# All 22 units of the up projection as seven products; the first two begin with their plain blocks

## The chip, the cores and the metric

One core of a Trainium2 chip runs one program. The metric is the time of one execution on the device, in microseconds (us); lower is better. The engines are named as in the profile: PE (matrix products; PEld is its weight load), DVE (vector), ACT (scalar), POOL, and SP, which here only issues DMAs. Each engine works through its own instructions in the order of the program and waits on semaphores for the others.

## The reference, cut to what matters

The kernel computes one layer over 1024 tokens of width 1024. The change lies in the last third: the residual stream after attention and retention is normed and modulated, and goes through a gated MLP with a depthwise convolution of width 3 over the tokens.

```
hx2 = _modulate(_rmsnorm(x, norm2_g[l]), sh2, sc2)
...
u = h @ w_up                       # (1024 x 1024) @ (1024 x 5632)
...
u = sum(up[:, i:i + n] * conv_w[i] for i in range(CONV_W)) + conv_b
a, val = jnp.split(u, 2, axis=-1)
return (jax.nn.silu(a) * val) @ w_down
```

## The kernel before

All large products are made in three matmuls each: an operand is split into a high part (a cast on ACT) and a low part (a subtraction on DVE), and high x high, high x low and low x high are summed in PSUM. `split` (L85 to L87) is that pair of instructions; a block of 128x512 weights that is to be used has to be loaded, cast and subtracted.

The 5632 columns of `w_up` are worked in 22 units of 2 x 128 columns, 128 of the gate branch and 128 of the value branch with the same number. `seq` gives their order: unit 0 is column block 0, unit 1 is block 11, unit 2 is block 1, and so on. A unit is a 2 x 2 block product: two branches by two halves of the depth (a11, a12 for the gate; a21, a22 for the value) times the normed rows h, in two halves of the depth by two halves of the tokens (B11, B21 for tokens 0 to 511, B12, B22 for tokens 512 to 1023).

- A **plain** unit multiplies all of it: 2 branches x 2 token halves x 8 depth blocks x 3 = 96 matmuls of 128x512. Units 0 and 1 are plain (`PLAIN = 2`, `up`).
- A **seven-product** unit (class `Seven`, `Up`) needs 7 products of 4 x 3 = 12 matmuls, 84 in all. It uses the sums S1 to S4 of its four weight blocks, made on POOL (L1388 to L1391, in this order, S2 and S4 each from the one before), and the combinations T1 to T4 of the four blocks of h. The products gather in the banks X, Y and Z of PSUM, are copied or added to SBUF between (p1, u2, u3; L1413, L1416, L1422, L1403), and the finished unit goes through `conv`. Units 2 to 21 are of this kind, interleaved.

Ahead of it, `out_proj(tb)` makes the output projection of token block tb (8 blocks of 128 tokens), the residual rows x1 and their norm; `norm_out(tb)` turns the normed rows on PE (L1663, two groups of four transposes), modulates them and writes the high and low parts of h. They are called as `out_proj(tb)`, `norm_out(tb - 1)`. For blocks 0 to 3, h is also stored to DRAM (`d_h`). For blocks 4 to 7 it is read back into the tile vo, and four subtractions (L1678 to L1681) make this block's share of T1 to T4, which is stored to DRAM (`d_t`). Later `comb` loads these shares, four per T, and splits them into the tiles T.

The order: unit 0's products with tokens 0 to 511 follow `norm_out(6)`, then come block 7's transposes, unit 0's second half, unit 1, the loads and splits of T, and unit 2. The order of instructions on each engine is set by the framework's scheduler from the program as it is written. SP issues nearly all DMAs in one queue: a DMA that waits for its buffer or its data holds up those behind it. Raw weight blocks, raw T shares and the sums S of the seven-product units share a ring of 12 buffers (`ur_load`, `Up.raw`, tag "r").

Of the kernel before, what the change touches and what calls it, by code (L numbers as in the profile page):

```python
# [40 lines left out]
def tile_hybrid_layer(ctx, tc: tile.TileContext, io, dbg=None):  # L41
# [1581 lines left out]
    op = sb("outp", "right")  # L1623
# [6 lines left out]
    def out_proj(tb):  # L1630
        half, ts = tb // 4, slice((tb % 4) * P, (tb % 4 + 1) * P)
        x1 = op.tile([P, D], F32, tag="x1", bufs=3, name="x1")
        xr = op.tile([P, D], F32, tag="xn", bufs=2, name="xn")
        sync.dma_start(x1, io["x"][tb * P : (tb + 1) * P])
        for dh in range(2):
            cs = slice(dh * 512, dh * 512 + 512)
            m = po.tile([P, 512], F32, tag="o", bufs=2, name="om")
            for kb in range(KB):
                wc = wo[kb, dh]
                h_, l_ = mg[kb, half]  # L1640
                mm3(m, h_[:, ts], l_[:, ts], wc[:, 0], wc[:, 1], kb == 0, kb == KB - 1)
            vec.tensor_tensor(xr[:, cs], m, gate1[:, cs], ALU.mult)
            vec.tensor_tensor(x1[:, cs], xr[:, cs], x1[:, cs], ALU.add)
        sync.dma_start(d_x1[tb * P : (tb + 1) * P], x1)
# [3 lines left out]
        pool.tensor_tensor(ss[:, 1:2], ss[:, 0:1], mhalf[:, 0:1], ALU.pow)  # L1648
        vec.tensor_scalar(xr, x1, ss[:, 1:2], None, ALU.mult)
        return xr  # L1650

    def norm_out(tb, xr):
# [7 lines left out]
        for kg in range(2):  # L1660
            tp = po.tile([P, 4, P], F32, tag="t", bufs=2, name="tp2")
            for k in range(4):
                pe.transpose(tp[:, k], xr[:, (kg * 4 + k) * P : (kg * 4 + k + 1) * P], ident)  # L1663
            for k in range(4):
                kb = kg * 4 + k
                t = h2[half][kb]
                h_, l_ = (t[:, 0, ts], t[:, 1, ts]) if half == 0 else (t[0][:, ts], t[1][:, ts])
                a, sh = a2[:, kb : kb + 1], col[:, 24 + kb : 25 + kb]
                act.activation(h_, tp[:, k], AF.Identity, bias=sh, scale=a)
                v = vr[:, kb]  # L1670
# [6 lines left out]
        (b11, b21), (b12, b22) = [(t[:, : KB // 2], t[:, KB // 2 :]) for t in (vo, vr)]  # L1677
# [4 lines left out]
        for c, t in enumerate((b11, b22, b12, b21)):  # L1682
            sync.dma_start(d_t[c, tb - 4], t)
# [9 lines left out]
    def up(u, wu, half):  # L1693
        h = h2[half]
        hi, lo = ([t[:, i] for t in h] if half == 0 else [t[i] for t in h] for i in range(2))
        mm_a(u[:, half * 512 : half * 512 + 512], wu, lambda k: hi[k], lambda k: lo[k])

    def up_load(j, br):
        return [wload(io["w_up"][j, br, i]) for i in range(2)]

# [3 lines left out]
    early = []  # L1704
    for br in range(2):
        early.append((u_tile(br), up_load(0, br)))
        up(*early[br], 0)
    norm_out(NTB - 1, xr)
    po.release()
    pu.append(ps("u_ps1", "left"))  # L1710
    op.release()
    wop.release()
    gpool[1].release()

# [3 lines left out]
    tap = sb("conv", "right")  # L1718
    cw = tap.tile([P, 2 * NF, 3], F32, name="cw")
    sync.dma_start(cw, io["conv_w"])  # L1720
    cb = tap.tile([P, 2 * NF], F32, name="cb")
    sync.dma_start(cb, io["conv_b"])
# [50 lines left out]
    def u_out():  # L1773
        return tap.tile([P, T], F32, tag="uu", bufs=4, name="uu")

    def comb(c):
        t = [tpl.tile([P, 4, KH, P], F32R, name=f"T{c}{i}") for i in range(2)]
        for b in range(4):
            if b % 2 == 0:
                pair = u_out()  # L1780
            raw = pair[:, b % 2 * 512 : b % 2 * 512 + 512]
            sync.dma_start(raw, d_t[c, b])
            split(t[0][:, b], t[1][:, b], raw.rearrange("p (k t) -> p k t", k=KH))
        return t

    combs = {}

    class Up(Seven):
# [12 lines left out]
        def banks(self):  # L1801
            t = u_tile(2 * self.n)
            self.X, self.Y = t[:, 0:512], t[:, 512:1024]
            self.Z = u_tile(2 * self.n + 1)[:, 0:512]
            self.u = [u_out() for _ in range(2)]
# [11 lines left out]
        def c11(self):  # L1817
            act.copy(self.dst(0, 0), self.X)

        def done(self, b, half):  # L1820
            if (b, half) == (0, 1):
                conv(self.j, *self.u)
# [11 lines left out]
    seq = [j + NH * i for j in range(NH) for i in range(2)]  # L1834
    PLAIN = 2
    units = [Up(n, j) for n, j in enumerate(seq)]
    units[PLAIN].load(with_vec)

    for n, j in enumerate(seq[:PLAIN]):
        us2 = []  # L1840
        for br in range(2):
            u, wu = (u_tile(2 * n + br), up_load(j, br)) if n else early[br]
            for half in range(2) if n else (1,):
                up(u, wu, half)
            us2.append(u)
        for c in ((1, 0), (2, 3))[n]:
            combs[f"T{c + 1}"] = comb(c)
        conv(j, *us2)
    units[PLAIN + 1].load()
    for i, n in interleaved(PLAIN, NF):  # L1850
        units[i].step(n)
# [237 lines left out]
```

## Time and profile before

| what | us |
|---|---|
| median of 3 runs (lowest to highest) | 1763.57 (1760.81 to 1767.86) |
| the profiled execution | 1769.98 |
| its span | 1768.2 |
| last output product done, block 6 turned | 1108.41 |
| first matmul of a seven-product unit | 1154.18 |
| up projection's last matmul | 1547 |

All times in timeline rows are us from the start of the span. In a timeline row stand the start, the duration, the engine, the line, the operation, the tiles written and read, and the number of like instructions in a row; in brackets the idle time of the engine before it, and what ended it. The rows on which the prediction rests stand in it.

### The profile page before, as it was taken

What the parts mean: (1) busy time and instruction counts of PE and PEld (TensorE: products, weight loads), DVE (VectorE), ACT (ScalarE), POOL (GpSimd) and SP (SyncE); (2) the same over time, 40 slices, a digit from 0 to 9 for tenths busy, and PEclk for the clock granted to TensorE, in tenths of its full rate; (3) what the DMA queues carried; (4) which work ended last, traced back from release to release, by engine and by line L of the source; (5) the groups of instructions that cost most, each with busy time, mean ns of one, the idle gap of its engine ahead of it and who ended that gap; (6) DMA issues with size and microseconds to landing.
All of it is one profiled execution on the core that took longest, in us unless ns stands there. A gap on an engine that the chain in (4) does not pass through costs nothing.

```text
span 1768.2 us, 24667 instructions
## 1 busy us (share of the span) xinstructions
PE 1722.8 (97%) x8357; PEld 1429.4 (81%) x8357; DVE 1305.5 (74%) x2458; ACT 851.4 (48%) x1833; POOL 571.0 (32%) x477
## 2 busy tenths in 40 slices
PE   8699999999999999999999999999999999999997
PEld 3588888888888888788888888878888888788886
DVE  4878888765776766777675557878899899876655
ACT  5666666653443434453444324534444444554444
POOL 2510000002233343555422400145555655111444
PEclk9899999999999999999999999999999999999999
DMA  9133433433232212576658643723322332586753
GB/s 345 48 118 118 125 111 121 141 101 124 75 91 59 81 39 81 171 244 229 215 186 296 216 150 140 258 101 98 111 90 91 119 119 90 167 298 192 243 167 148
DMA packets 139551, 261.61 MB, mean 148 GB/s; under 512 B 15872, under 2 KB 28320, under 8 KB 139424
## 3 DMA queue, kind: packets, MB, share of 16 engines
q1 hardware_dynamic: 121504, 239.05, 41.2%
q10 hardware_dynamic: 17920, 20.98, 3.4%
q8 instruction: 66, 1.08, 0.3%
q14 instruction: 61, 0.50, 0.1%
HBM read 187.87 MB, written 69.48 MB: 146 GB/s over the span
## 4 chain that ended last, share of the span: by engine, by line
PE 44%; issue 5%; POOL 3%; DVE 3%; DMA 1%; ACT 1%; SPq 0%; POOLq 0%; ACTq 0%; DVEq 0%
PE u L1374 29%; PE y L1374 4%; PE pr L111 2%; PE pr L110 2%; PE pr L112 2%; PE om L121 1%; PE om L123 1%; PE om L122 1%; POOL x L1903 1%; PE pn L112 1%; PE pn L110 1%; PE pn L111 1%; DMA vo<-d_h 1%; DVE wc L87 0%; DMA uu<-d_t 0%
## 5 line engine op out<-in xcount | busy, mean ns | idle before, releaser
L1374 PE MATMUL u<-T,wc 128*128 128x512 f32 x960 | 228.6, 394 | 4.2 <-ACT pu L1413 2.6
L1374 PEld LDWEIGHTS u<-T,wc 128*128 128x128 f32 x960 | 181.2, 190 | 45.9 <-ACT pu L1413 5.9
L1374 PE MATMUL y<-wc,ahl 128*128 128x512 f32 x924 | 212.1, 391 | 2.9 <-DVE wc L87 1.8
L1374 PEld LDWEIGHTS y<-wc,ahl 128*128 128x128 f32 x924 | 174.4, 189 | 40.2 <-DVE wc L87 2.5
L87 DVE TENSOR_TENSOR wc<-ur,wc 128x512 fp32r<-128x512 f32 x137 | 124.6, 911 | 62.0 <-ACT wc L86 62.0
L86 ACT CAST wc<-ur 128x512 fp32r<-128x512 f32 x137 | 85.1, 622 | 126.9 <-PE y L1374 72.1
L111 PE MATMUL mm<-low,wc 128*128 128x512 f32 (+1 forms) x328 | 123.9, 378 | 0.0
L1374 PE MATMUL u<-h2a,wc 128*128 128x512 f32 x480 | 112.4, 389 | 0.7 <-DVE pu L1422 0.7
L110 PE MATMUL mm<-hx,wc 128*128 128x512 f32 x264 | 107.4, 407 | 0.3 <-DVE vc L221 0.3
L1374 PEld LDWEIGHTS u<-h2a,wc 128*128 128x128 f32 x480 | 90.0, 188 | 19.8 <-DVE pu L1422 1.2
L112 PE MATMUL mm<-hx,wc 128*128 128x512 f32 x264 | 105.0, 398 | 0.0
L86 ACT CAST wc<-s 128x512 fp32r<-128x512 f32 x80 | 49.7, 622 | 90.4 <-PE u L1374 87.4
L1513 POOL TENSOR_TENSOR col<-col,bcol 128x32 f32<-128x32 f32 x1 | 0.3, 253 | 282.2 <-DVE aw L538 282.2
L123 PE MATMUL mm<-wc,low 128*128 128x512 f32 (+1 forms) x240 | 91.3, 380 | 0.0
L1374 PE MATMUL u<-hxT,wc 128*128 128x512 f32 x384 | 89.6, 389 | 0.0
L87 DVE TENSOR_TENSOR wc<-s,wc 128x512 fp32r<-128x512 f32 x80 | 84.4, 1055 | 5.4 <-ACT wc L86 5.1
L1374 PEld LDWEIGHTS u<-hxT,wc 128*128 128x128 f32 x384 | 72.1, 188 | 15.0
L87 DVE TENSOR_TENSOR wc<-raw,wc 128x512 fp32r<-128x512 f32 x92 | 68.8, 757 | 17.1 <-ACT wc L86 17.0
L121 PE MATMUL mm<-wc,hx 128*128 128x512 f32 x192 | 75.2, 392 | 0.6 <-ACT r L1105 0.6
L122 PE MATMUL mm<-wc,hx 128*128 128x512 f32 x192 | 75.2, 392 | 0.0
L86 ACT CAST wc<-raw 128x512 fp32r<-128x512 f32 x92 | 56.7, 621 | 32.3 <-DMA raw<-in_w_pret 6.8
L87 DVE TENSOR_TENSOR wc<-wr,wc 128x512 fp32r<-128x512 f32 x56 | 54.2, 972 | 21.7 <-ACT wc L86 21.5
(393 smaller groups left out, 4693.2 us busy)
## 6 DMA issues: line engine op xcount, KB each, us to landing
ur<-in_w_up SPq DMA_DIRECT2D x80, 256.0 KB, 2.9
ur<-d_a SPq DMA_DIRECT2D x77, 256.0 KB, 3.4
aw<-in_w_ada SPq DMA_DIRECT2D x32, 512.0 KB, 3.2
pj<-in_w_down SPq DMA_DIRECT2D x44, 256.0 KB, 4.4
d_w<-pj SPq DMA_DIRECT2D x44, 256.0 KB, 2.0
d_a<-sa SPq DMA_DIRECT2D x44, 256.0 KB, 2.0
ur<-d_w SPq DMA_DIRECT2D x44, 256.0 KB, 3.6
d_a<-at SPq DMA_DIRECT2D x33, 256.0 KB, 2.8
```

The source lines that it names most:

```text
L86: act.copy(hi, src)
L87: (lo_eng or vec).tensor_tensor(lo, src, hi.bitcast(F32), ALU.subtract)
L110: pe.matmul(out, wh, xh, start=k == 0, stop=False)
L111: pe.matmul(out, wh, xl, start=False, stop=False)
L112: pe.matmul(out, wl, xh, start=False, stop=k == n - 1)
L121: pe.matmul(out, ah, bh, start=first, stop=False)
L122: pe.matmul(out, ah, bl, start=False, stop=False)
L123: pe.matmul(out, al, bh, start=False, stop=last)
L1374: pe.matmul(out, a, b, start=first and n == 0, stop=last and n == 2, skip_group_check=True)
L1513: pool.tensor_tensor(col[:, 16:48], col[:, 16:48], bcol[:, 16:48], ALU.add)
L1903: pool.tensor_tensor(z, z, fg[:, gs(dh)], ALU.mult)
```

## The change

Units 0 and 1 become seven-product units too. They begin with what needs only tokens 0 to 511: `early_plain` makes a11 x B11 in bank X, copies it (p1), and adds a12 x B21 in the same bank, for unit 0 and then for unit 1. The weight blocks for these two products are loaded and split ahead, through `wload`. Then `units[0].load()` loads the four blocks again for the sums, `norm_out(7)` turns block 7 into the free bank Z of unit 0, and its share of T1 to T4 is split where it is made, without going through DRAM. The other twelve shares are loaded through the ring of 12 buffers (before, through tiles of the convolution) and split, and `units[1].load()` follows. `open` copies the finished part in bank X to the unit's result (c11) and makes S4 x B22 in that bank; `close` makes the four products with T1 to T4 and the sums that differ by this order. The five remaining products of units 0 and 1 are written alternating, with unit 2's first product among them.

In `norm_out`, the group of depth blocks 4 to 7 comes first, and for tokens 512 to 1023 the depth blocks 0 to 3 are no longer split (no product uses them plain any more): ACT writes them to v in one instruction each. The tile x1 has two buffers in place of three.

```diff
-        x1 = op.tile([P, D], F32, tag="x1", bufs=3, name="x1")
+        x1 = op.tile([P, D], F32, tag="x1", bufs=2, name="x1")
...
-            h2[1] = [(gtile(0, F32R, "h2h"), gtile(0, F32R, "h2l")) for _ in range(KB)]
+            h2[1] = [None] * KH + [(gtile(0, F32R, "h2h"), gtile(0, F32R, "h2l")) for _ in range(KH)]
...
-        for kg in range(2):
-            tp = po.tile([P, 4, P], F32, tag="t", bufs=2, name="tp2")
+        for kg in (1, 0):
+            tp = banks[kg].rearrange("p (k t) -> p k t", k=4) if banks else po.tile([P, 4, P], F32, tag="t", bufs=2, name="tp2")
...
+                if t is None:
+                    act.activation(v, tp[:, k], AF.Identity, bias=sh, scale=a)
+                    continue
...
         for c, t in enumerate((b11, b22, b12, b21)):
-            sync.dma_start(d_t[c, tb - 4], t)
+            if banks:
+                split(combs[f"T{c + 1}"][0][:, tb - 4], combs[f"T{c + 1}"][1][:, tb - 4], t)
+            else:
+                sync.dma_start(d_t[c, tb - 4], t)
...
+    def early_plain(n):
+        X = early[n][0][:, 0:512]
+        early_prod(X, n, 0)
+        p1 = gtile(0, F32, "pu")
+        act.copy(p1, X)
+        early_prod(X, n, 1)
+        return p1
...
+        def open(self):
+            self.banks()
+            self.p1 = early_p1[self.n]
+            self.c11()
+            self.prod(self.X, self.s4, "B22", True, True)
+
+        def close(self, n):
+            if n == 0:
+                self.prod(self.Z, self.s1, "T1", True, True)
+            elif n == 1:
+                self.u2, self.u3 = (self.tmp() for _ in range(2))
+                self.prod(self.Y, self.s2, "T2", True, False)
+                vec.tensor_tensor(self.u2, self.Y, self.p1, ALU.add)
+                vec.tensor_tensor(self.u2, self.X, self.u2, ALU.add)
+                self.add(0, 1, self.Z, self.u2)
+            elif n == 2:
+                self.prod(self.Y, self.s3, "T3", False, False)
+                vec.tensor_tensor(self.u3, self.Y, self.p1, ALU.add)
+                self.add(1, 1, self.Z, self.u3)
+            else:
+                self.prod(self.Y, self.a22, "T4", False, True)
+                self.add(1, 0, self.Y, self.p1)
...
+    units[0].load()
+    for c in ("T1", "T2", "T3", "T4"):
+        combs[c] = [tpl.tile([P, 4, KH, P], F32R, name=f"{c}{i}") for i in range(2)]
+    norm_out(NTB - 1, xr, (early[0][1][:, 0:512], early[0][1][:, 512:1024]))
+    for c in (0, 1, 2, 3):
+        hi, lo = combs[f"T{c + 1}"]
+        for b in range(3):
+            raw = ur_load(d_t[c, b])
+            split(hi[:, b], lo[:, b], raw.rearrange("p (k t) -> p k t", k=KH))
...
+    units[1].load()
+    units[0].open()
+    units[1].open()
+    for i, n in ((0, 0), (1, 0), (0, 1), (1, 1), (0, 2), (0, 3), (1, 2), (2, -1), (1, 3)):
```

What this does to the order on three engines, at the start of the up projection. In the rows of the change, u_11859 and u_11860 are unit 0's banks (X and Y; Z), u_11903 and u_11904 unit 1's; xn_11760 are block 7's normed rows; wc is a split weight block, s a raw sum and ur a raw block.

PE in the change, from block 6's last transposes on:

```order
L1663 MATMUL tp2_11842<-ident_76,xn_11660 128x128 x4
L1374 MATMUL u_11859<-h2a_11035,wc_11863 128x512 x3
...
L1663 MATMUL u_11860<-ident_76,xn_11760 128x128 x4
L1374 MATMUL u_11859<-h2a_11039,wc_11882 128x512 x3
...
L1374 MATMUL u_11903<-h2a_11035,wc_11907 128x512 x3
...
L1374 MATMUL u_11903<-h2a_11039,wc_11926 128x512 x3
...
L1663 MATMUL u_11860<-ident_76,xn_11760 128x128 x4
L1374 MATMUL u_11859<-h2h_11614,wc_12085 128x512
...
L1374 MATMUL u_11903<-h2h_11614,wc_12103 128x512
L1374 MATMUL u_11903<-h2l_11615,wc_12103 128x512
L1374 MATMUL u_11860<-T10_11963,wc_12118 128x512
```

and before, where block 7 is turned behind 48 matmuls of unit 0:

```order
L112 MATMUL u_11926<-h2a_11042,wc_11934 128x512
L1663 MATMUL tp2_11964<-ident_76,xn_11784 128x128 x4
L1663 MATMUL tp2_11981<-ident_76,xn_11784 128x128 x4
L110 MATMUL u_11891<-h2h_11614,wc_11894 128x512
L110 MATMUL u_11926<-h2h_11614,wc_11929 128x512
```

Block 7's first group of transposes has moved from behind 48 matmuls to behind 12, its second group to behind 48; the products with h of tokens 512 to 1023 (h2h, h2l) now need S4 of units 0 and 1 (wc_12085, wc_12103).

ACT in the change, from the cast of unit 0's S4 to that of unit 1's (13 casts of T stand between block 7's four activations and the copy uu_12082):

```order
L86 CAST wc_12085<-s_11958 128x512
L1718 COPY pu_11922<-u_11903 128x512
...
L1670 ACTIVATE v_11971<-u_11860,col_83,a2_8902 128x128 x4
L86 CAST T10_11963<-ur_12018 128x512
L86 CAST T10_11963<-vo_11972 128x512
...
L86 CAST T40_11969<-ur_12046 128x512
L86 CAST T40_11969<-ur_12050 128x512
L1839 COPY uu_12082<-u_11859 128x512
L1839 COPY uu_12100<-u_11903 128x512
L86 CAST T40_11969<-ur_12054 128x512
L86 CAST wc_12103<-s_12077 128x512
L86 CAST wc_12118<-s_11955 128x512
```

and before, where the casts of T stand among the convolution of unit 0 and behind unit 2's first weight casts:

```order
L86 CAST wc_12330<-ur_12030 128x512
L86 CAST wc_12346<-s_12035 128x512
L1751 ACTIVATE ta_12123<-u_11891,cb_12024,cw_12022 128x1024
L86 CAST T10_12090<-uu_12092 128x512 x2
L1751 ACTIVATE at_12122<-u_11926,cb_12024,cw_12022 128x1024
```

Two copies out of PSUM (pu_11922, uu_12082) and the cast of unit 1's S4 now stand in one row with the casts of T.

SP in the change, from unit 0's first weight load on (d_x1 is the store of the residual rows, vo the read of `d_h`):

```order
L1738 DMA ur_11947<-in_w_up 128x512
L1659 DMA vo_11823<-d_h_65 128x1024
L1644 DMA d_x1_59<-x1_11759 128x1024
L1738 DMA ur_11949<-in_w_up 128x512
L1738 DMA ur_11951<-in_w_up 128x512
L1689 DMA d_t_66<-vo_11823 128x512
L1738 DMA ur_11953<-in_w_up 128x512
...
L1738 DMA ur_12050<-d_t_66 128x512
L1738 DMA ur_12054<-d_t_66 128x512
...
L1738 DMA ur_12066<-in_w_up 128x512
L1738 DMA ur_12068<-in_w_up 128x512
```

Unit 0's fourth block, A12 (ur_11953), stands behind a store of block 6's share of T1 (vo_11823); unit 1's blocks (ur_12066 and on) stand behind all twelve loads of T shares.

More of the change, by code (lines that the diff above doesn't have):

```diff
@@ L1818, in c11 @@
             act.copy(self.dst(0, 0), self.X)
+            self.done(0, 0)
         def done(self, b, half):
-            if (b, half) == (0, 1):
+            self.left -= 1
+            if self.left == 0:
                 conv(self.j, *self.u)
```

86 lines of the change are left out of this document (34 added, 52 removed).

## The prediction

> **What bounds the kernel now.** I read first the page's busy shares and its costliest groups, then the waits, then the stretch around the start of the up projection by windows and by timeline, TensorE's first.
>
> ```profile
> PE 1722.8 (97%) x8357; PEld 1429.4 (81%) x8357; DVE 1305.5 (74%) x2458; ACT 851.4 (48%) x1833; POOL 571.0 (32%) x477
> ...
> L1374 PE MATMUL u<-T,wc 128*128 128x512 f32 x960 | 228.6, 394 | 4.2 <-ACT pu L1413 2.6
> ```
>
> TensorE (PE) is busy 97% of the span: whoever saves time saves products, or closes one of the few places where PE stands. The changed stage has such a place.
>
> ```profile
> 1107.62 1.04 PE L1663 MATMUL tp<-ident,xn 128*128 128x128 f32 x8
> 1108.41 0.48 PE L110 MATMUL u<-h2a,wc 128*128 128x512 f32 x1
> ...
> 1156.90 0.61 PE L1374 MATMUL u<-T,wc 128*128 128x512 f32 x2
> 1159.06 0.73 PE L1374 MATMUL u<-T,wc 128*128 128x512 f32 x2 [1.55 <-DVE wc L87]
> 1162.40 10.23 PE L1374 MATMUL u<-T,wc 128*128 128x512 f32 x32 [2.60 <-ACT pu L1413]
> 1172.47 5.60 PE L1374 MATMUL u<-h2a,wc 128*128 128x512 f32 x24
> 1177.91 8.32 PE L1374 MATMUL u<-T,wc 128*128 128x512 f32 x36
> 1186.07 0.39 PE L1374 MATMUL u<-h2h,wc 128*128 128x512 f32 x1
> ```
>
> The timeline of PE. From 1177.91 to 1186.07, 36 matmuls take 8.16 us: **0.2267 us each** undisturbed, so a product of 12 matmuls is 2.72 us. From 1108.41 (first plain product) to 1172.47 PE did two plain units (192 matmuls), four products of the third (48) and 8 transposes (1108.41 - 1107.62 = 0.79): 240 x 0.2267 + 0.79 = 55.2 us of work in 64.06. **8.9 us are lost there**, in waits and in the clock:
>
> ```profile
> 1140.00:1162.40 22.40, 18.25 (x81) 14.46 (x79) 21.90 (x25) 16.17 (x26) 4.62 (x3) 0.98 0.52 169
> 1160.00:1165.00 5.00, 2.60 (x6) 2.12 (x7) 5.00 (x8) 2.57 (x4) 0.00 (x0) 0.63 0.61 193
> 1165.00:1170.00 5.00, 5.00 (x17) 3.90 (x17) 2.47 (x3) 0.67 (x2) 4.80 (x3) 0.68 0.47 174
> ```
>
> The windows (length, then busy time of PE, PEld, DVE, ACT, POOL, the granted clock, DMA): DVE is full (21.90 of 22.40) with the splits of the combinations T while PE waits, and after the wait the clock falls. The 32 matmuls from 1162.40 took 10.07 us where 7.25 were due: 2.8 us by the clock.
>
> **The change, part by part.** *Fewer products.* Two units go from 96 matmuls to 84: 24 x 0.2267 = **5.4 us less** on PE, the one certain gain. With the 8.9 us above it could be 14.3, if PE never stood. So I follow the new order of each engine through this stage, on before's clock, from 1108.41, where the first product on rows 0 to 511 can start in both kernels.
>
> *Wait 1, transposes.* Block 7's first four transposes stood behind 48 matmuls and now stand behind 12: PE reaches them at 1108.41 + 2.72 = 1111.1.
>
> ```profile
> 1083.87 0.25 PE om L123
> 1084.12 0.02 issue
> 1084.14 0.70 DVE xn L1642
> ...
> 1087.71 0.75 DVE xn L1649
> ```
>
> The chain from a block's last output product to its scaled rows takes 1088.46 - 1084.12 = 4.3 us when nothing is in its way. Block 7's last product ends at about 1107.8, so its rows are there at 1112.1 at the earliest; before's crowded DVE had them at 1113.28 + 0.75:
>
> ```profile
> 1113.28 0.75 DVE L1649 TENSOR_SCALAR xn<-x,ss 128x1024 f32<-128x1024 f32 x1 [0.44 <-POOL ss L1648]
> ```
>
> DVE is relieved of eight small instructions per block here, so I take 1112.3: PE waits 1.2 us (1.0 to 2.9). Four transposes (0.4) and the next 24 matmuls then end at 1118.1.
>
> *Wait 2, the bank of unit 1.* Its B21 product adds onto the bank that ACT must first copy (pu_11922), and in ACT's order that copy stands behind the cast of unit 0's S4. S4 is the last of four POOL sums and needs A12, whose load stands on SP behind a store of block 6's combinations, which wait for rows read back from DRAM.
>
> ```profile
> 1108.73 0.32 SPq L1683 DMA_DIRECT2D d_t<-vo  x1
> 1109.14 0.87 SPq L1727 DMA_DIRECT2D ur<-in_w_up  x2
> 1110.85 0.33 SPq L1644 DMA_DIRECT2D d_x<-x  x1
> ...
> 1111.27 6.10 DMA vo<-d_h
> ...
> 1123.30 3.25 DMA vo<-d_h
> ```
>
> ```profile
> ur<-in_w_up SPq DMA_DIRECT2D x80, 256.0 KB, 2.9
> ...
> d_w<-pj SPq DMA_DIRECT2D x44, 256.0 KB, 2.0
> ```
>
> The buffer vo comes free when block 5's store (1108.73) has landed, with the 2.0 us of the nearest store at 1110.7; the read takes 3.25 to 6.10: 1114.0 to 1116.8. The combination and the store's issue add about 1 us, A12's landing 2.9: 1118 to 1120.7. Beside that, the second weight block now stands behind the store of x at 1110.85: issued about 1111.7, landed at 1114.6 or later.
>
> ```profile
> 1130.16 1.61 POOL L1388 TENSOR_TENSOR s<-ur 128x512 f32<-128x512 f32 x1 [16.91 <-DVE vo L1681]
> ...
> 1134.67 1.73 POOL L1391 TENSOR_TENSOR s<-ur,s 128x512 f32<-128x512 f32 x1
> ...
> 1161.77 0.58 ACT L1413 COPY pu<-u 128x512 f32<-128x512 f32 x1
> ```
>
> The four sums take 1136.40 - 1130.16 = 6.2 us, so S4 is there between 1120.9 and 1122.5; I take 1122.0. ACT's cast (0.53, below) and copy (0.58) let B21 start at 1123.2: **PE waits 5.1 us** (3.9 to 5.6).
>
> *Wait 3, the bank of unit 0.* B21 and four transposes end at 1123.2 + 2.72 + 0.4 = 1126.3. The next product, B22 of unit 0, overwrites the bank that ACT copies into uu_12082. In ACT's order this copy stands behind four activations of block 7's other half and 13 casts of T.
>
> ```profile
> 1108.26 0.90 ACT L1669 ACTIVATE h2h<-tp,col,a 128x128 fp32r<-128x128 f32 x2 [2.36 <-PE tp L1663]
> 1144.84 3.73 ACT L86 CAST T<-uu 128x512 fp32r<-128x512 f32 x7
> 1141.29 2.49 DVE L87 TENSOR_TENSOR T<-uu,T 128x512 fp32r<-128x512 f32 x4
> 1149.61 7.60 DVE L87 TENSOR_TENSOR T<-uu,T 128x512 fp32r<-128x512 f32 x7
> ```
>
> 4 x 0.45 + 13 x 0.53 + 0.58 = 9.3 us: B22 starts at 1135.6, and **PE waits 9.3 us**. The last of these casts reads a buffer that DVE's split of an earlier T must free: DVE starts the combination at 1128.1, frees it at about 1129.5, the load lands 3 to 5 us later, inside the 13 casts. So the wait is 9 at the least, 11 with slow loads.
>
> *Wait 4, unit 1's weights.* All raw blocks share 12 buffers. Unit 0 still holds four, so unit 1's four weight loads come on SP behind the twelve T loads and wait for DVE's splits. From 1128.1 DVE has 18 instructions (4 combinations, 14 splits), at 2.49 / 4 = 0.62 us each with POOL idle. The buffer of the second weight load comes free behind the eleventh (so the order of the buffers has it) at 1128.1 + 11 x 0.62 = 1134.9; the load is issued at 1135.3 and lands 2.9 later, at 1138.2. POOL's sums take 5.2 (four at the 1.30 of a lone one) to 6.2, so S4 of unit 1 is there at 1144.0, cast at 1144.6. B22 of unit 0 was done at 1138.3: **PE waits 6.3 us** (4 to 8). Queued behind that cast on ACT are all the other weight casts, behind the T splits on DVE the weight splits, and on SP the loads of unit 2.
>
> ```profile
> 1133.42 1.30 POOL L1390 TENSOR_TENSOR s<-ur 128x512 f32<-128x512 f32 x1
> ```
>
> *After it.* At 1144.6 PE has done 60 of the first three units' 252 matmuls. Before had 36 of its 276 left at 1172.47. 156 x 0.2267 = 35.4 gives 1180.0. A restart after a stall cost before 2.8 us by the clock; I take the same: 1182.8, against 1172.47: **+10.3 us**. Weight splits (0.62 to 1.09 each, the last two rows above) keep ahead of products of 2.72: nothing more (0 to 2).
>
> *The clock after wait 2.* Before, the clock fell to half when PE had done four matmuls between 1157.5 and 1162.40. 5.1 us of standing should do the same, and B21's 12 matmuls at half clock push everything behind them by 2.7: **+13.0**. The Trainium skill, page "TensorE: Matmul & The Clock Gate", section "Part 1: The HAM clock gate (the "warmup" mystery)", asks for one whole idle window of about 3.4 us on a free-running grid; by that, 5.1 us holds such a window in about half of the phases, and the sum would be +10.3 or +13.0 by luck. The trace speaks for less than a whole window: two waits of 1.55 and 2.60 us with matmuls between them were enough. I keep +13.0.
>
> ```profile
> 1085.59 0.32 SPq L1644 DMA_DIRECT2D d_x<-x  x1
> ...
> 1107.41 0.68 DVE L1643 TENSOR_TENSOR x<-xn,x 128x512 f32<-128x512 f32 x1
> ```
>
> *At nothing:* one buffer of x fewer: block 7's load now waits for block 5's store, issued at 1085.59, and its rows are first used at 1107.41; the 22 us between, filled with block 6's and 7's output products, hide it (without that cover it would cost one load, some 4 us). Four DMAs fewer, and small norm instructions moved to ACT, which is 48% busy: nothing.
>
> Check: 1.2 + 5.1 + 9.3 + 6.3 = 21.9 new waits + 2.8 + 2.7 clock - 8.9 old losses - 5.4 = +13.1. The profiled execution (1769.98, span 1768.2) would be 1783; it was 6.4 above the median 1763.57, so I put the same difference on the median: **1777 us**, +0.75%.
>
> **The rivals.** *Not slower, the feed comes early* (other side): if unit 1's four loads went out before the T loads, S4 of both units were there by 1122, ACT's casts would be the only queue, and waits 3 and 4 shrink below the 8.9 us that before loses. At the best all waits go: -14.3, **1749**. It decides at new waits of 8.9 + 5.4 = 14.3. Against it: SP's order puts the loads behind, and ACT's 13 casts cannot end before 1135 unless block 7's transposes come earlier. *Early S4:* if A12 and the second weight block land by 1115, S4 is there at 1119.5; wait 2 is 2.6, the clock holds, and all behind comes 2.5 sooner: 10.3 - 2.5 = +7.8, **1771**, within 0.5%. For it: loads at 2.9 are a median. *Clock holds* after 5.1 us: +10.3, **1774**. *Slow splits:* at 7.60 / 7 = 1.09 us, if POOL runs beside them, 11 of them until the weights add 5: +18, **1782**.
>
> **How the numbers follow.** A difference of 0.5% (8.8 us, about what a measurement of this kernel can tell from none) starts at 1772.4. Forecast 0.38, clock holds 0.25, slow splits 0.10: slower together 0.73. Early S4, with other mixtures of shorter waits, 0.20 within 0.5%. The feed in time 0.07, faster. Range 1766 to 1785: above it only slow splits with more clock loss (0.05), below it the early feed and the lucky end of early S4 (0.12).
>
> **What would show it.** PE's count falls by 24. PE stands before the B21 of unit 1 (released by ACT's pu copy), before its first matmul on B22 of unit 0 (ACT's uu copy) and before B22 of unit 1 (ACT's cast of s), some 5, 9 and 6 us; the granted clock shows half speed behind the first or second of them; from unit 1's B22 on no wait is over 1 us. I am wrong if ACT's uu copy comes before 1131 on this clock, or if unit 1's S4 is there before 1138.

## The result and the profile after

The changed kernel takes **1783.56 us** (median of 4 runs, 1780.95 to 1786.32), the kernel before, run beside it, 1765.14 (4 runs, 1760.81 to 1767.86): ratio **1.0107**, 95% interval 1.0079 to 1.0135. A second series of runs gave 1784.33 against 1766.96, ratio 1.0092 (1.0070 to 1.0113). The change makes the kernel slower by about 1%, 12 to 24 us. The profiled execution took 1782.43 (span 1780.0), 12.4 more than that of before.

The page's first part, busy time of each engine:

```profile
PE 1722.8 (97%) x8333; PEld 1427.2 (80%) x8333; DVE 1309.6 (74%) x2444; ACT 853.6 (48%) x1843; POOL 581.7 (33%) x485
```

PE has 24 matmuls fewer, 5.4 us of work, and is busy just as long as before (1722.8), because other matmuls took longer. About 3 us of that is in the next rows: 5.8 us are lost there by slow matmuls, 2.8 in the prediction's rows of before. The rest lies outside these rows: ahead of them, with the same matmuls, PE was busy 1082.6 us here and 1079.4 before. The timeline of PE through the start of the up projection, after (start, busy time, instruction, in brackets the idle time ahead and what ended it):

```profile
1109.00 2.98 PE L1374 MATMUL u<-h2a,wc 128*128 128x512 f32 x12
1112.90 0.66 PE L1663 MATMUL u<-ident,xn 128*128 128x128 f32 x4 [0.92 <-DVE xn L1649]
...
1122.35 4.37 PE L1374 MATMUL u<-h2a,wc 128*128 128x512 f32 x12 [3.30 <-ACT pu L1718]
1126.56 0.60 PE L1663 MATMUL u<-ident,xn 128*128 128x128 f32 x4
1136.86 0.79 PE L1374 MATMUL u<-h2h,wc 128*128 128x512 f32 x1 [9.71 <-ACT uu L1839]
...
1146.14 0.79 PE L1374 MATMUL u<-h2h,wc 128*128 128x512 f32 x1 [3.79 <-ACT wc L86]
...
1150.64 15.57 PE L1374 MATMUL u<-T,wc 128*128 128x512 f32 x68
...
1559.99 20.34 PE L1374 MATMUL y<-wc,ahl 128*128 128x512 f32 x89
```

Four waits of 0.92, 3.30, 9.71 and 3.79 us, released by the four things that the prediction named, 17.7 us in all; behind them no wait in this stage is over 0.8 us. Behind three of the four the matmuls start at about half speed: the 12 of B21 take 4.21 us (1122.35 to 1126.56) where 2.72 are due, the 12 of unit 0's B22 5.49 (1136.86 to 1146.14 - 3.79), the 13 matmuls from 1146.14 to 1150.64 take 4.50 where 2.95 are due. That is 5.8 us more.

I call **the stage** the time from the first plain product to the long run of y products, the start of the down projection: 1559.99 - 1109.00 = 451.0 us here, 1546.90 - 1108.41 = 438.5 before (1546.90 is the row below). All of the profiled pair's difference of 12.4 us is in it (12.5).

```profile
1546.90 33.48 PE L1374 MATMUL y<-wc,ahl 128*128 128x512 f32 x147
```

Where VectorE stood meanwhile: windows of after, then of before (length, busy time of PE, PEld, DVE, ACT, POOL, granted clock, DMA):

```profile
1120.00:1140.00 20.00, 7.94 (x23) 6.18 (x24) 15.84 (x28) 12.70 (x25) 1.16 (x1) 0.72 0.74 251
1140.00:1160.00 20.00, 16.21 (x61) 12.68 (x60) 11.40 (x12) 5.71 (x10) 12.73 (x9) 0.86 0.38 121
```

```profile
1120.00:1140.00 20.00, 19.33 (x86) 15.53 (x85) 14.36 (x29) 8.89 (x16) 7.42 (x5) 1.00 0.67 229
1140.00:1160.00 20.00, 18.25 (x80) 14.46 (x78) 19.50 (x22) 14.07 (x22) 4.62 (x3) 1.00 0.52 171
```

In the changed kernel no engine is full in either 20 us: PE 7.94 of 20, DVE 15.84 and then 11.40. Everybody waits for somebody. Before, the plain products kept PE at work (19.33, 18.25) while DVE caught up on the splits of T. The chain of waits of after, followed from 1120 to unit 1's B22 (start, duration, what):

```profile
1121.31 0.60 DVE vo L1684
...
1121.94 2.00 DMA d_t<-vo
...
1123.95 5.24 DMA vo<-d_h
...
1129.27 0.70 DVE vo L1681
...
1137.40 2.95 DMA ur<-in_w_up
...
1144.22 1.23 POOL s L1391
```

Between the last DVE row and the weight load (ur) stand ACT's casts of T, and behind the sum s its cast (1145.47) and PE's matmul. This is one queue through VectorE, the DMAs, ScalarE and GpSimd, with PE as its last member. The prediction had one of its links in front of wait 2 but not here: there is a single buffer vo, so the stored rows with which block 7 is combined can be read back (5.24 us) only when block 6's last combination has been stored from it (2.00 us). But this link came last by only 0.5 us: the read landed at 1129.19, and ACT's four activations on block 7, behind PE's transposes, ended at 1128.69. ACT's timeline:

```profile
1127.19 1.50 ACT L1670 ACTIVATE v<-u,col,a 128x128 f32<-128x128 f32 x4 [0.85 <-PE u L1663]
1128.58 0.63 ACT L86 CAST T<-ur 128x512 fp32r<-128x512 f32 x1
1130.00 0.62 ACT L86 CAST T<-vo 128x512 fp32r<-128x512 f32 x1 [0.80 <-DVE vo L1681]
...
1136.24 1.05 ACT L1839 COPY uu<-u 128x512 f32<-128x512 f32 x2
```

From 1127.19 on stand four activations, 13 casts and the first uu copy, back to back but for the 0.80 us in which ACT waits for block 7's first combination. PE starts B22 behind that copy, at 1136.86.

### The profile page after: what moved, and what is told of

Read it like the earlier page. It is cut to its first block, busy times and chain, and to the rows that moved or that the text cites. A ratio compares the mean times of both kernels' runs of the same rounds, so it can differ in the third digit from the quotient of the medians.

```text
span 1780.0 us, 24636 instructions
## 1 busy us (share of the span) xinstructions
PE 1722.8 (97%) x8333; PEld 1427.2 (80%) x8333; DVE 1309.6 (74%) x2444; ACT 853.6 (48%) x1843; POOL 581.7 (33%) x485
## 3 DMA queue, kind: packets, MB, share of 16 engines
q8 instruction: 65, 1.06, 0.2%
## 4 chain that ended last, share of the span: by engine, by line
PE 44%; issue 5%; DVE 3%; POOL 3%; ACT 1%; DMA 1%; POOLq 0%; ACTq 0%; DVEq 0%; SPq 0%
PE u L1374 29%; PE y L1374 4%; PE om L121 2%; PE om L122 2%; PE om L123 2%; PE pr L111 2%; PE pr L110 2%; PE pr L112 2%; POOL x L1935 1%; PE pn L112 1%; PE pn L111 1%; PE pn L110 1%; DVE wc L87 1%; DVE ta L1763 0%; DVE at L1763 0%
## 5 line engine op out<-in xcount | busy, mean ns | idle before, releaser
L1374 PE MATMUL u<-T,wc 128*128 128x512 f32 x1056 | 248.5, 391 | 1.3 <-DVE pu L1416 0.8
L1374 PEld LDWEIGHTS u<-T,wc 128*128 128x128 f32 x1056 | 197.5, 188 | 46.1 <-ACT pu L1413 3.1
L1374 PE MATMUL u<-h2a,wc 128*128 128x512 f32 x528 | 126.0, 393 | 4.1 <-ACT pu L1718 3.3
L1374 PEld LDWEIGHTS u<-h2a,wc 128*128 128x128 f32 x528 | 99.7, 190 | 26.3 <-ACT pu L1718 3.7
L86 ACT CAST wc<-s 128x512 fp32r<-128x512 f32 x88 | 54.1, 621 | 103.7 <-PE u L1374 92.2
L87 DVE TENSOR_TENSOR wc<-s,wc 128x512 fp32r<-128x512 f32 x88 | 90.7, 1036 | 6.3 <-ACT wc L86 5.9
L1388 POOL TENSOR_TENSOR s<-ur 128x512 f32<-128x512 f32 x22 | 34.8, 1582 | 121.8 <-DVE wc L87 77.4
L1374 PE MATMUL u<-h2h,wc 128*128 128x512 f32 x176 | 60.9, 407 | 13.5 <-ACT uu L1839 9.7
```

Of the source, the lines that this page charges most:

```text
L86: act.copy(hi, src)
L87: (lo_eng or vec).tensor_tensor(lo, src, hi.bitcast(F32), ALU.subtract)
L1374: pe.matmul(out, a, b, start=first and n == 0, stop=last and n == 2, skip_group_check=True)
L1388: pin(pool.tensor_tensor(self.s1, self.a21, self.a22, ALU.add))
```

## The experiments

Theory Q (a queue): the time at which T and unit 1's S4 are fed decides, and PE's waits are only the places where that shows; taking one wait away lengthens the next. Its rivals: the waits add up (A), the clock makes the loss (C), T and VectorE's splits hold behind everything (D), GpSimd's sums and VectorE slow each other (V). Executions differ by some us ahead of the stage too, so the stage, taken from each kernel's profile, is the measure, beside the ratio of the timed runs to those of the kernel before:

| kernel | stage, us | ratio to before (95%) |
|---|---|---|
| before; once more (e12) | 438.5; 435.9 | |
| after; once more (e8) | 451.0; 453.0 | 1.0107 (1.0079 to 1.0135); 1.0092 (1.0070 to 1.0113) |
| e1 copy first | 453.2 | 1.0103 (1.0086 to 1.0120) |
| e2 blocks aside | 451.7 | 1.0087 (1.0070 to 1.0103) |
| e3 loads first | 449.3 | 1.0066 (1.0049 to 1.0082) |
| e4 clock kept | 451.4 | 1.0080 (1.0061 to 1.0098) |
| e5 = e2 + e3 | 448.9 | 1.0060 (1.0038 to 1.0083) |
| e6 = e5 + third unit | 446.0 | 1.0062 (1.0042 to 1.0083) |
| e7 = e6 + e1 + block 6 | 439.2 | 1.0034 (1.0018 to 1.0049) |
| e9 sums on VectorE | 446.3 | 1.0065 (1.0044 to 1.0085) |
| e10 = e7 + sums | 435.9 | 1.0023 (1.0010 to 1.0035) |
| e11 before + sums | 435.0 | 1.0004 (0.9989 to 1.0019) |

The stage comes from one profile of each run. Two executions of one kernel differ in it by 2.6 us (before) and 2.0 (after), so a difference of that size between two rows says little by itself.

### e1: unit 1's copy ahead of the cast (wait 2)

```
-        act.copy(p1, X)
+        early_copy.append(act.copy(p1, X))
...
-            self.prod(self.X, self.s4, "B22", True, True)
...
+            cast = act.copy(w[:, 0], self.s4)
+            tc.add_manual_dep(cast.ins, early_copy[1].ins.name, mybir.DependencyInfo(mybir.DependencyClass.NoSync, mybir.DependencyReason.DATA))
...
```

> Edit: on ScalarE, unit 1's bank copy (pu) goes ahead of the cast of unit 0's S4, so the second new wait has no cause any more. Theory Q (one queue: what counts is when the combinations T and the second S4 are fed; the time at which PE reaches its earlier products is not what holds): B21 of unit 1 starts by 1120 on the changed kernel's clock and at full clock, the wait of 3.3 us is gone, but the wait for the uu copy grows by what was won (9.7 to 12 to 14 us), since that copy stays behind the same T casts; the time changes by 0 to -2.5 us. Rival A (the waits add up one by one): -3.3 and the 1.6 us that B21 lost at half clock, -5 us.

Neither. The stage is 453.2, as long as in the changed kernel. ScalarE's timeline in e1:

```profile
1119.48 0.46 ACT L1673 ACTIVATE h2h<-u,col,a 128x128 fp32r<-128x128 f32 x1 [3.53 <-DVE v L1674]
1123.04 0.46 ACT L1673 ACTIVATE h2h<-u,col,a 128x128 fp32r<-128x128 f32 x1 [3.10 <-DVE v L1674]
1123.40 0.58 ACT L1718 COPY pu<-u 128x512 f32<-128x512 f32 x1
```

The cast no longer stands ahead of the copy, but two activations of block 7 do, which wait for VectorE, 3.53 and 3.10 us: the copy came at 1123.40, 13.6 us after the first product (1109.82), in the changed kernel 12.7 (1121.71 - 1109.00). So the edit did not do what it was made for, and it says nothing on A. What it shows is that the cast was not the only thing in ScalarE's row.

### e2: finished blocks copied aside (wait 3)

```
         early_prod(X, n, 1)
+        c0 = gtile(0, F32, "pu")
+        act.copy(c0, X)
+        early_c11.append(c0)
...
-            self.c11()
...
                 self.prod(self.Z, self.s1, "T1", True, True)
+                act.copy(self.dst(0, 0), early_c11[self.n])
+                self.done(0, 0)
```

> Edit: the finished upper left blocks of units 0 and 1 are copied aside right behind their second product into a spare buffer and moved to uu later, so B22 of unit 0 no longer waits for the uu copy behind the T casts (wait of 9.7 us). Theory Q: B22 of unit 0 runs by 1128 and then PE stands once, 14 to 17 us, for the cast of unit 1's S4, which stays near 1145.5; the time changes by -1 to +1 us. Rival A (the waits add up): -9.7 us and the 2.6 us that B22 of unit 0 lost at half clock, -12 us.

PE's timeline in e2:

```profile
1118.76 0.80 PE L1374 MATMUL u<-h2h,wc 128*128 128x512 f32 x1 [2.71 <-ACT wc L86]
...
1119.78 4.04 PE L1374 MATMUL u<-h2a,wc 128*128 128x512 f32 x12
...
1142.63 0.79 PE L1374 MATMUL u<-h2h,wc 128*128 128x512 f32 x1 [16.05 <-ACT wc L86]
```

The 9.71 us are gone, B22 of unit 0 is done by 1126.6, and PE stands 16.05 us for unit 1's S4. That wait ends 36.6 us after the first product (1106.01), in the changed kernel 37.1. Theory Q's numbers came out, and the stage is unchanged (451.7); A wanted 12 us.

### e3: unit 1's loads ahead of the T loads (wait 4)

```
     units[0].load()
+    units[1].load()
...
-            raw = ur_load(d_t[c, b])
+            raw = rawload(d_t[c, b]) if (3 * c + b) % 2 else ur_load(d_t[c, b])
...
-    units[1].load()
```

> Edit: unit 1's four weight loads and sums go out directly behind unit 0's, ahead of the T loads; every other T load lands in a buffer of the other stream of raw blocks, since the ring of 12 is full. Theory Q: S4 of unit 1 is cast by 1132 in place of 1145.5, the wait of 3.8 us behind B22 of unit 0 is gone, the wait for the uu copy (9.7) stays within 3 us of its size because ScalarE's T casts stay ahead of it, and up to 3 us of waits for T come anew; the time changes by -4 to -7 us. Rival D (the T splits on VectorE are the bound behind everything): the same wait comes back in front of the first T product, 0 to -2 us.

```profile
1122.12 4.81 PE L1374 MATMUL u<-h2a,wc 128*128 128x512 f32 x12 [5.57 <-ACT pu L1718]
...
1134.22 1.22 PE L1374 MATMUL u<-T,wc 128*128 128x512 f32 x2 [6.85 <-ACT T L86]
```

PE's timeline in e3. Unit 1's S4 is no longer waited for; wait 2 grew from 3.30 to 5.57, and T is waited for in place of the uu copy, 6.85 us and then 2.37 for its split on VectorE. The stage is 1.7 to 3.7 us shorter than in the two executions of the changed kernel, between D's 0 to 2 and Q's 4 to 7; by the medians, each against that of the kernel before beside it, the gain is 6 to 7 us, Q's. The two measures do not agree well enough to decide here.

### e4: the clock kept up through waits 3 and 4

```
         def open(self):
             self.banks()
...
+            for k in range((30, 22)[self.n]):
+                m = pe.matmul(early[1][1][:, 512:1024], w[:, 0, 0:P], w[:, 0], start=True, stop=True)
...
```

> Edit: 30 idle products into an unused half bank between block 7's last transposes and B22 of unit 0, and 22 ahead of B22 of unit 1 (matmuls that add no term of the result): PE is busy inside the third and fourth wait, and the clock should be full behind both. Theory Q: B22 of unit 0 ends 2 to 3 us sooner and the wait for unit 1's S4 takes that in; only B22 of unit 1 is won, which now takes 4.5 us for 12 products: -1.8 us. Rival C (the clock makes the loss): all that B22 of both units lose at half clock comes back, -4.4 us or more.

```profile
1136.36 0.50 PE L1374 MATMUL u<-h2h,wc 128*128 128x512 f32 x1 [2.65 <-ACT uu L1844]
...
1145.63 0.50 PE L1374 MATMUL u<-h2h,wc 128*128 128x512 f32 x1 [1.27 <-ACT wc L86]
...
1148.76 15.80 PE L1374 MATMUL u<-T,wc 128*128 128x512 f32 x69
```

Both B22 run at full clock, the 12 matmuls of the second in 3.13 us (1145.63 to 1148.76). But it starts 37.1 us after the first product (1108.56), to a tenth as in the changed kernel: what the first B22 won, the queue took. What is left, 1.1 us (1.55 lost behind wait 4 in the changed kernel, 0.4 here), did not show in the whole stage (451.4). By the medians, each against that of the kernel before beside it, e4 gains 3.4 to 4.5 us, with intervals that overlap, so how much of the time came back is not settled. Even C's full 4.4 us would be a quarter of the slowdown: C is out as the main cause. Of the 5.8 us that matmuls lost to the clock in the changed kernel, the 2.8 between waits 3 and 4 did not move unit 1's B22.

### e5, e6: two waits together, and more work for PE

e5 is e2's and e3's diffs together. e6 adds unit 2's two plain products in an unused half bank:

```
-        X = early[n][0][:, 0:512]
+        X = early[n][0][:, 0:512] if n < EARLY else early[1][1][:, 512:1024]
...
+    early_p1.append(early_plain(2))
...
```

> The edits of e2 (finished blocks copied aside) and e3 (unit 1's loads ahead of the T loads) together. Loss of PE is counted from the first plain product to the first product of the fourth unit (less 156 products of 0.2267 us and 0.8 us of transposes): 25.0 us in the changed kernel, 24.7 in e2, 22.5 in e3. Theory Q (one queue: ScalarE's T casts and the feed of unit 1's S4 each hide the other): together they win more than their sum of 2.8 us, 7 to 10 us, so a loss of 15 to 18 us and a time 7 to 11 us below the changed kernel's on this chip. Rival A (gains add): 2.8 us, loss 22.2. Rival D (what holds is that T is not ready, whatever else is ready): no more than e3's 2.5 us.

> e5, and the two plain products of unit 2 brought forward too (into an unused half bank), so PE has 24 more products that need no T. Theory Q: 24 products of 0.2267 us fill up to 5.4 us of what e5 still loses; since two of its waits lie ahead of them or come with their banks, 1 to 4 us less loss than e5. Rival D (T holds): the waits for T shrink by just what is brought forward, up to 5.4 us. Rival E (ScalarE's copies for the third unit delay its T casts): nothing, within 1 us of e5.

The expectation speaks of the fourth unit's first product; the 156 products that it counts end at that of the third (unit 2), and so it is counted here. In e5 that product starts at 1167.96, so the loss is 1167.96 - 1108.97 - 156 x 0.2267 - 0.8 = 22.8 us: 2.2 less than in the changed kernel, not 7 to 10. **Theory Q fails here**; A's sum of two small gains (2.8) and D's bound (2.5) both fit the number. PE's timeline and DVE's window in e5:

```profile
1133.61 0.51 PE L1374 MATMUL u<-h2h,wc 128*128 128x512 f32 x1 [1.31 <-ACT wc L86]
...
1140.96 12.11 PE L1374 MATMUL u<-T,wc 128*128 128x512 f32 x45 [1.53 <-DVE T L87]
1157.05 11.07 PE L1374 MATMUL u<-T,wc 128*128 128x512 f32 x36 [3.98 <-DVE pu L1822]
```

```profile
1140.00:1160.00 20.00, 15.05 (x52) 11.91 (x53) 19.95 (x25) 9.01 (x15) 9.98 (x7) 0.81 0.46 136
```

PE reaches unit 1's B22 12 us earlier than in the changed kernel (24.6 against 37.1 us after the first product), and then loses it: VectorE is full (19.95 of 20) with splits of T and of weights, so its sum out of the bank (L1822) comes late, PE stands 3.98 us for it, and the next 36 matmuls start at half clock (10.91 us to 1167.96 where 8.16 are due). Behind the queue stands VectorE's work: D in a wider form. In e6 the stage is 2.9 us shorter, within Q's 1 to 4; PE's 24 matmuls brought forward would fill time in which VectorE works. But by the medians the two are alike, and 2.9 is hardly more than two executions of one kernel differ: this gain is not shown.

### e7: everything, and block 6 split where it is made

e7 is e6 with e1's edit, and with block 6's `norm_out` moved behind unit 0's loads, where the tiles T exist already, and the plain products and unit 1's loads behind it:

```
-            if banks:
+            if tb >= NTB - 2:
                 split(combs[f"T{c + 1}"][0][:, tb - 4], combs[f"T{c + 1}"][1][:, tb - 4], t)
...
+    norm_out(NTB - 2, last)
...
-        for b in range(3):
...
+        for b in range(2):
...
```

> e6, and unit 1's bank copy ahead of the cast of unit 0's S4 (e1), and the combinations of block 6 split where they are made as well (no store and no read back of them; eight T loads instead of twelve). Theory Q: both the S4 casts and T come sooner; PE's loss from the first plain product to the first product of the fourth unit is 11 to 14 us, no wait over 2.5 us is left and the clock holds through the stage; the time is 10 to 15 us below the changed kernel's and within 0.3% of the kernel before. Rival F (VectorE is full there and slowed by GpSimd's sums, so more splits early push the rest back): no better than e6.

The stage is 439.2, 12 to 14 us shorter than in the changed kernel, the time 1772.08 against 1784.33. The loss up to unit 3's first product (1173.35, behind 228 products) is 10.8 us, where 11 to 14 was expected; but waits of 3.71 and 3.26 are left, and the clock drops once. DVE's windows say what holds now:

```profile
1120.00:1140.00 20.00, 15.40 (x62) 11.95 (x61) 19.96 (x30) 14.75 (x30) 6.83 (x5) 0.91 0.44 150
1140.00:1160.00 20.00, 18.60 (x80) 14.19 (x79) 17.86 (x23) 7.18 (x13) 14.74 (x8) 1.00 0.37 109
```

### e8 and e12: both kernels once more

> The changed kernel as it is, beside the others on one chip. If the gap of 12.4 us between the two profiled executions is the change's size, the ratio is 1.007 (+12 us); if the gap of the medians is, 1.0107 (+19 us).

> The kernel before once more, for a second profile of it. If the two waits of 1.55 and 2.60 us and the half clock behind them belong to the kernel, the stage is 438.5 us again, within 0.7; if they come and go from execution to execution, it is 3 us or more shorter here, which would explain why the medians lie 17 to 19 us apart and the first pair of profiled executions 12.4.

In e8 the four waits are there again (0.92, 3.19, 9.17 and 4.24 us), with other clock losses. PE at the second of them, and VectorE at block 7's first combination:

```profile
1121.35 5.49 PE L1374 MATMUL u<-h2a,wc 128*128 128x512 f32 x12 [3.19 <-ACT pu L1718]
1129.11 0.69 DVE L1681 TENSOR_TENSOR vo<-v,vo 128x512 f32<-128x512 f32 x1 [2.61 <-ACT v L1670]
```

B21's 12 matmuls took 5.29 us (1121.35 to 1126.64), 1.1 more than in the first execution behind a wait of nearly the same length; the stage is 453.0. And block 7's combination here waited for ACT's activations, not for vo: which of the two comes last changes from one execution to the next. In e12, the kernel before again:

```profile
1157.35 0.73 PE L1374 MATMUL u<-T,wc 128*128 128x512 f32 x2 [0.42 <-DVE wc L87]
1160.68 8.90 PE L1374 MATMUL u<-T,wc 128*128 128x512 f32 x32 [2.60 <-ACT pu L1413]
1169.42 5.60 PE L1374 MATMUL u<-h2a,wc 128*128 128x512 f32 x24
```

The wait of 2.60 is the same, the other is 0.42 and not 1.55, and the 32 matmuls take 8.74 and not 10.07. The stage is 435.9, 2.6 us shorter than in the execution on which the prediction was made: nearly the 3 us of the expectation's second reading. The difference of the two kernels' stages is thus 12.5 to 17.1 us over these four executions, 14.8 in the mean. That lies within the ratio's interval (12.4 to 20.0 us in the second series). What lies outside the stage took 1325.4 to 1331.2 us of the span in the profiles of these kernels, without an order that has to do with the edits; whether the 3 us that are left between 14.8 and the medians' 17 to 18 are only that spread stays open.

### e9, e10, e11: the weight sums on VectorE

VectorE's timeline after, beside GpSimd's four sums (1115.0 to 1121.2):

```profile
1114.52 0.28 DVE L1675 TENSOR_TENSOR h2l<-v,h2h 128x128 fp32r<-128x128 f32 x1
...
1116.58 1.77 DVE L1682 TENSOR_TENSOR v<-v 128x512 f32<-128x512 f32 x1
1118.27 0.40 DVE L1674 TENSOR_SCALAR v<-u,a,col 128x128 f32<-128x128 f32 x1
...
1119.96 1.34 DVE L1675 TENSOR_TENSOR h2l<-v,h2h 128x128 fp32r<-128x128 f32 x1
1121.23 0.68 DVE L1684 TENSOR_TENSOR vo<-vo,v 128x512 f32<-128x512 f32 x1
```

Subtractions of two SBUF tiles take 1.3 to 1.8 us there and 0.28 or 0.68 a moment earlier or later; the TENSOR_SCALAR out of PSUM keeps its 0.40. The edit of e9, also that of e11 (for units 2 and 3 there, `< 4`) and of e10 (`< 3`, on e7):

```
+            eng = vec if type(self).__name__ == "Up" and self.n < 2 else pool
...
-            pin(pool.tensor_tensor(self.s1, self.a21, self.a22, ALU.add))
+            pin(eng.tensor_tensor(self.s1, self.a21, self.a22, ALU.add))
...
```

> The changed kernel with the four weight sums of units 0 and 1 on VectorE in place of GpSimd. In the changed kernel VectorE's two-input instructions took 1.3 to 1.8 us beside these sums where 0.7 is usual, and GpSimd took 6.1 us for the four. Theory V (GpSimd's sums and VectorE slow each other, and both lie on the queue that feeds S4 and T): four sums take 2.7 us on VectorE, its other instructions are back at 0.7, S4 of unit 0 is there 2 to 4 us sooner, so B21 of unit 1 waits under 1.5 us in place of 3.3, and S4 of unit 1 comes 2 to 4 us sooner too; the stage (from the first plain product to the first product of the down projection, 451.0 and 453.0 us in two executions of the changed kernel) is 2 to 6 us shorter. Rival W (VectorE is short of time in this stage, so eight more instructions of 0.7 there lengthen it): 0 to 4 us longer.

> All edits of e7, and the sums of units 0, 1 and 2 on VectorE. In e7 VectorE was busy 48.1 of the 52 us from 1108 to 1160, with T splits of 1.8 us beside GpSimd's sums, so it was the bound there. Theory V: its slowed instructions cost about 7 us beside the first eight sums, and the eight sums cost it 5.5, so VectorE gains 1 to 2 us and S4 comes sooner: the stage is 2 to 4 us shorter than e7's 439.2, i.e. 435 to 437, and shorter than the 438.5 of the kernel before; the time 0 to 0.3% under the kernel before. Rival W: VectorE is full, 0 to 3 us longer than e7.

> Control: the kernel before with the sums of its first two seven-product units on VectorE, nothing else. If e10 wins only through these sums, this kernel wins as much: its stage, 438.5 us in one execution, would be 2 to 4 us shorter. Theory V for the kernel before: its wait of 2.6 us and the clock drop behind it (2.8 us) follow splits of T that ran at 1.1 us beside GpSimd's sums, so up to 5 us can go. Rival W: VectorE was busy all the time from 1140 to 1160 there, so the sums push PE's wait by 1 to 3 us more.

PE's and DVE's timelines in e9:

```profile
1120.71 3.02 PE L1374 MATMUL u<-h2a,wc 128*128 128x512 f32 x12 [0.68 <-ACT pu L1719]
...
1135.09 0.79 PE L1374 MATMUL u<-h2h,wc 128*128 128x512 f32 x1 [10.91 <-ACT uu L1840]
...
1142.26 0.80 PE L1374 MATMUL u<-h2h,wc 128*128 128x512 f32 x1 [2.41 <-ACT wc L86]
```

```profile
1116.53 0.69 DVE L1683 TENSOR_TENSOR v<-v 128x512 f32<-128x512 f32 x1
1117.13 0.68 DVE L1389 TENSOR_TENSOR s<-ur 128x512 f32<-128x512 f32 x1
```

The combinations are back at 0.69, the sums take 0.68 each, B21 waits 0.68 us and runs at full clock, and unit 1's B22 starts 32.3 us after the first product (1109.99) in place of 37.1. The stage is 4.7 to 6.8 us shorter: V, not W. By the stage it is the largest gain of a single edit; by the medians e3's ratio is the same (1.0066 and 1.0065).

In e10 no wait is over 2.0 us and the clock holds through both windows:

```profile
1120.00:1140.00 20.00, 17.73 (x78) 14.21 (x79) 19.87 (x38) 16.65 (x34) 0.00 (x0) 1.00 0.50 151
1140.00:1160.00 20.00, 19.15 (x84) 15.08 (x83) 19.89 (x28) 9.09 (x11) 7.47 (x5) 1.00 0.33 99
```

Its stage, 435.9, is as expected, 15 to 17 us shorter than the changed kernel's, and exactly that of the kernel before in e12. Its time was expected under that of the kernel before and is not: 1.0023 (1.0010 to 1.0035). VectorE is full in both windows, and PE, with 5.4 us less work in a stage of the same length, stands that much longer. In e11 the same edit frees the kernel before of its two waits (36 matmuls on T run from 1161.25 in one piece). But another wait grows ahead of them, for the low part of block 7's rows from VectorE (1.76 us at 1124.58, 0.56 before), with slow matmuls behind it. The stage is 435.0, 0.9 us below e12's, and the time does not move measurably: 1.0004 (0.9989 to 1.0019). No version beat the kernel before.

## Why the prediction was right, and where its sizes were off

**What bounds the kernel, and the direction: right.** The 24 products were worth their 5.4 us, and the new waits at the start of the up projection cost more. The four waits were where the prediction put them and released by what it named.

**The terms**, predicted and measured in the first profile: wait 1, 1.2 and 0.92; wait 2, 5.1 and 3.30 (unit 0's S4 was there at 1121.16, or 1120.6 on before's clock, where 1122.0 was taken; the four sums took 6.1 us, where 6.2 was given, but began sooner); B21 at half clock, 2.7 and 1.5; wait 3, 9.3 and 9.71; wait 4, 6.3 and 3.79; the restart, 2.8 and 1.55. One term was missing, the 2.8 us that unit 0's B22 lost at half clock behind wait 3. With wait 4 they make 6.6, near the 6.3 predicted for wait 4 alone, since S4 of unit 1 decides when both are over: it was there at 1145.45, less 0.59 for the later start 1144.9, and predicted for 1144.0. e2 and e4 show that this is no accident: whenever PE gets through unit 0's B22, that of unit 1 starts 36.6 to 37.1 us after the first product.

**That the sum came so close is in part luck.** Wait 2 was 1.8 us shorter than forecast, and B21 lost 1.5 us behind it; so PE reached wait 3 at 1126.6 on before's clock, where the working without the clock loss had 1126.3 and the one that was kept, 2.7 us later, 1129.0. Up to unit 2's first product PE lost 25.0 us (the count of e5's expectation) where 21.9 + 2.8 + 2.7 = 27.4 were forecast. Behind that product the stage took 389.85 us for 1692 matmuls, in the kernel before 374.43 for 1632: 1.8 us more than the 60 matmuls account for, where the prediction had 0 to 2 and took nothing. What makes these 1.8 us was not looked into. The two misses nearly cancel: 25.0 + 1.8 - 8.9 - 5.4 = 12.5.

**The mechanism of wait 3 held.** The uu copy stood behind four activations and 13 casts in ScalarE's row, and they took what was forecast. What the prediction did not have here is the read into vo. It made some 0.5 of the 0.80 us for which that row stood in the first execution; in e8 the row stood for 0.25 and the read was not the last to come. In e9, where the transposes come 4 us sooner, the read is the last to come, and wait 3 is 10.91. A buffer of its own for vo was not tried alone.

**GpSimd beside VectorE** was priced in one rival only (slow T splits, 1782) and missed where it bit, in the combinations of block 6 and the sums of unit 0. e9 puts its price in the changed kernel at 4.7 to 6.8 us of the stage. The Trainium skill's page "GPSIMD Engine Reference", section "8. Key points", says that GpSimd shares its SBUF interfaces with VectorE and collides with VectorE's instructions on two SBUF inputs; the rows above agree, for the slowed ones are those and not the TENSOR_SCALAR out of PSUM.

**The clock.** The prediction kept a drop after wait 2, and it came in both executions, after 3.30 and 3.19 us; in e2 2.71 us were enough, right behind 24 matmuls without a gap. In the prediction's rows of before it is two matmuls, not four, that stand between 1157.5 and 1162.40; its reading of them holds. The Trainium skill, page "TensorE: Matmul & The Clock Gate", section "Part 1: The HAM clock gate (the "warmup" mystery)", asks for a whole idle window of about 3.4 us. The e2 row does not agree with that: any 3.4 us there held 0.7 us of work or more, so a wholly idle window was not needed.

**The size.** The step that failed is "I put the same difference on the median", 1777, where 1783.56 was measured. For the profiled pair the sum gave +13.1, and +12.4 was measured. But the 8.9 us that the kernel before loses there belong to that execution: in e12 they are 1169.42 - 1108.05 - 55.2 = 6.2. With 6.2 the sum is 13.1 + 2.7 = +15.8. That gives 1781 on the median of the kernel before in the first series (1765.14), where 1783.56 was measured for the changed one, and 1783 on that in the second (1766.96), where 1784.33 was: 1.5 to 2.6 us are left open. The clock losses on both sides of the difference were taken from one execution, and they move: 2.8 and 1.5 us in the two executions of the kernel before, 5.8 and 7.4 in those of the changed one.

**The rivals.** Clock holds, early S4 (half of it: S4 came 1.4 us sooner than taken, not 2.5) and slow splits did not come out as cases of their own. The other side, an early feed, was tried: e3, e5 and e7 feed S4 and T sooner, and with e10 all new waits of any size are gone. The best that it gave is the time of the kernel before plus 0.2%, not 1749. What that rival left out, by e10's windows, is VectorE: it is full there (19.87 and 19.89 of 20), so that its work finds no room without the plain products. That nothing else holds e10 is argued, not shown.

## What to carry to other kernels

A product that seems superfluous may be the cover under which another engine gets its work done: before taking it out, add up what that engine must finish by the time at which the saved product's successor needs it. When an engine waits several times in a row, ask which of the waits ends at a time that its own earlier work does not move (here unit 1's S4, 37 us after the start, in three kernels): only that one can be worth an edit, and behind it may stand the next engine's full load (here e3 and e5 fed S4 sooner and won little). Where a difference is made of stalls that trip the clock, take its terms from more than one execution before putting the sum on a median.

## What was not expected of the hardware

- A VectorE subtraction of two SBUF tiles beside GpSimd's sums took about 1.06 us more whatever its size: 0.28 became 1.34 for 128x128, 0.68 became 1.77 for 128x512. That looks like waiting for one GpSimd instruction (1.26 us when alone) rather than a lower rate. Four sums on VectorE (0.68 each, 2.7 us) were cheaper for VectorE itself than four on GpSimd, which lengthened five of its subtractions by 3.9 us.
- The length of a wait alone does not tell whether the clock drops: 2.71 us did it in e2 (12 matmuls in 3.88 us, 1119.78 to 1123.66), 3.19 in e8, while 3.26 us in e7 left the next 12 at 2.98, at full clock:

```profile
1195.88 2.98 PE L1374 MATMUL u<-h2a,wc 128*128 128x512 f32 x12 [3.26 <-DVE pu L1422]
```
